# Three quarters of a depthwise convolution moved from VectorE to TensorE, and two thirds of its norm moved to an earlier stage

## The chip, the cores and the metric

The kernel runs on one core of a Trainium2 chip. The metric is the device time in microseconds (us) of one execution. Three runs of the kernel before took 2881.78 us in the median (2876.07 to 2883.0).

## The reference

One step of a two-layer encoder over 1024 prompt tokens and 8 x 16 sample tokens, 1152 in all, model width 1024. Layer 0 has stick-breaking attention (8 heads of 64) and, in parallel, a convolution module over 512 channels; layer 1 has banded attention with 16 heads; each layer is followed by a squared-ReLU MLP of width 4096. Everything is float32. The part that the change touches:

```python
def conv_module(u_ext, dw_w, dw_b, ln_g, ln_b):      # dw_w: 31 taps x 512 channels
    y = lax.conv_general_dilated(u_ext, dw_w[:, None, :], ..., feature_group_count=CONV_CH) + dw_b
    return jax.nn.silu(layernorm(y, ln_g, ln_b))

q, k, v, a, g = jnp.split(h @ w_in, [...])           # ab_project
u = a * jax.nn.sigmoid(g)
u_ext = jnp.concatenate([cache_conv, u], axis=1)      # 30 old rows, zeros for the prompt
out = jnp.concatenate([a_out, c_out], axis=-1) @ w_out
```

The convolution is depthwise: each of the 512 channels has its own 31 taps along the tokens. The layer norm goes over the 512 channels. The last 30 rows of u are outputs too.

## The kernel before

Activations lie with 128 channels on the partitions and the 1152 tokens along the free axis, in three groups of 384 (`G`). A matmul of high precision is made of three fp32r matmuls over a high and a low half of each operand (`SPLIT`); `split` makes the halves, one on ScalarE (L180) and one on VectorE (L181). Weights come through SP's queue into three staging buffers `st` (`staging`, L187), are split into `hl` buffers and used by `dense` (L220). `weights_ahead` keeps one chunk of 128 output channels loaded ahead.

Layer 0's mixer is `mixer0`. `start` loads the tokens, normalises them and projects the first two of the four chunks of u (gate and value). Then comes the projection of head pair 0, and then four rounds, p = 0 to 3. Round p expands q, k and v of its pair, runs 8 jobs of attention (`attend`: scores L864 to L867, sigmoids L868 and L869, a scan and a product on VectorE L847 and L849, transposes L392, splits, weighted sums L404) and the attention of the sample tokens, and has beside it the projection of pair p + 1 as `fill`. Rounds 0 and 1 project also the u chunks 2 and 3 (`ag`); round 3 has instead the first part of the output projection (`part_out`, tiles psoa).

The convolution is `tap`: for each of 4 chunks and 31 taps two VectorE instructions (L671), y = u x w + y, one over the 1024 prompt tokens and one over the 128 sample tokens. There are 124 such steps; `TAPS` shares them out, 26 beside the first projection and 36, 38 and 24 in rounds 0, 1 and 2. The finished chunk goes to DRAM (`cat_d`, L674 and L675). `conv_norm`, in round 3, loads all four chunks of a token group back (L955), takes the mean with plain fp32 matmuls against ones (L961), centres (L963), squares, makes 1/std (`rstd_of`, L258 and L280) and scales, applies SiLU, and splits the result into `cat_t`, from which the output projection reads.

The order is written by two planners. `merge` interleaves lists of `Step`s by their planned TensorE time, so that each list advances in proportion; a step may name another that it comes `after`, with a `lag` in ns. `level` spreads extra VectorE steps (the taps) over a list by planned VectorE time. Each engine then runs its instructions in that order. DMAs issued by `dma` stand in SP's queue, those of `put` in POOL's; both are in order.

Of the kernel before, what the change touches and what calls it, by code (L numbers as in the profile page):

```python
# [15 lines left out]
P = 128  # L16
D = 1024
KC = 8
T = 1152
TP = 1024  # L20
TAPS = (26, 36, 38, 24)
# [10 lines left out]
UW = UP + 8 * US  # L32
NF = 32
# [86 lines left out]
def tile_trunk(ctx, tc, ins, outs):  # L120
# [26 lines left out]
    dw = const.tile([P, 4, CW], F32, name="dw")  # L147
    cvec = const.tile([P, 3, 4], F32, name="cvec")
    for t, n in ((norms, "norms"), (dw, "dw"), (cvec, "cvec")):
        (nc.scalar.dma_start if n == "norms" else put)(t, ins[n])  # L150
# [23 lines left out]
    xr_d = [dram.tile([KC, P, T], F32, name=f"xr_d{l}") for l in range(2)]  # L174
    hid_d = [dram.tile([NF, P, T], F32, name=f"hid_d{l}") for l in range(2)]

# [415 lines left out]
    def mixer0():  # L592
        with ExitStack() as st:
# [28 lines left out]
            us, ys, tapped = {}, {}, [0] * 4  # L622
            conv_pool = ExitStack()
            cv = Bufs(conv_pool.enter_context(pool("conv")), u=2, y=1)

            def gate(c, ps, g):
                if g == 0:
                    assert c < 2 or tapped[c - 2] == CW
                    us[c] = cv.tile([P, UW], F32, "u", f"u{c}")
                    nc.gpsimd.memset(us[c][:, 0:CW - 1], 0.0)  # L630
                    dma(us[c][:, UP:].rearrange("p (b t) -> p b t", t=US)[:, :, 0:CW - 1], ins["conv_in"][:, c])
# [8 lines left out]
            def u_parts(c, ps, g):  # L640
                n = G if g < 2 else TP - 2 * G
                o = CW - 1 + g * G
                parts = [(us[c][:, o:o + n], ps[:, :n], rstd[g][:, :n])]
                if g == 2:
                    parts.append((us[c][:, UP:].rearrange("p (b t) -> p b t", t=US)[:, :, CW - 1:],
                                  ps[:, n:G].rearrange("p (b t) -> p b t", t=16), None))
                return parts

            def value(c, ps, g):
                for dst, src, _ in u_parts(c, ps, g):  # L650
                    tt(dst, src, dst, ALU.mult)
                if g == 2:
                    put(outs["conv_p"][c], us[c][:, TP:UP])
                    put(outs["conv_s"][c], us[c][:, UP:].rearrange("p (b t) -> p b t", t=US)[:, :, 16:])

            def tap(c, j):
                if j == 0:
# [5 lines left out]
                          u[:, UP:].rearrange("p (b t) -> p b t", t=US)[:, :, j:j + 16]))  # L663
# [13 lines left out]
            taps = [Step(0.0, lambda c=c, j=j: tap(c, j), 1340.0) for c in range(4) for j in range(CW)]  # L677
# [225 lines left out]
            run(level(proj(0), taps[:TAPS[0]]))  # L903
            taps = taps[TAPS[0]:]
            carry, cat_t = [], None
            for p in range(4):
                S["p"] = p
                expand_qk(p)
                if p < 3:
                    fill = proj(p + 1)  # L910
                    if p < 2:
                        fill[10:10] = ag(p + 2)
                    n = TAPS[p + 1]
                    mix, now, taps = [], taps[:n], taps[n:]
                else:
                    cat_t = new_hs("cat0")
                    (first, fill), now = part_out(0, range(3), pp, cat_t), []
                    for s in taps:
                        s.pe = 900.0
                    mix = taps + conv_norm(lambda: (conv_pool.close(), Bufs(st.enter_context(pool("ln")), t1=3, yl=5))[1],  # L920
                                           cat_t)
                cat = Cat(0, p, wk, cat_t)
# [15 lines left out]
                run(level(merge(steps, sample, fill, mix), now))  # L938
            return cat_t

    def conv_norm(new_pool, cat_t):

        steps = []
# [3 lines left out]
        def norm(g):  # L947
            box = {}

            def load():  # L950
# [3 lines left out]
                for c in range(4):  # L954
                    put(box["y"][c], cat_d[0][4 + c, :, g * G:g * G + G])  # L955
# [19 lines left out]
            def out(c):  # L975
# [7 lines left out]
                split(cat_t[g][1][0][:, c, :], cat_t[g][1][1][:, c, :], y)  # L983
# [3 lines left out]
                     Step(2600.0, centre, 1900.0, f"c{name}", f"l{name}", 4000), Step(500.0, squares, 1400.0),  # L987
                     Step(700.0, scale, 1200.0, f"s{name}", f"c{name}", 5000),
# [731 lines left out]
```

## Time and profile before

| what | us |
|---|---|
| median of three runs | 2881.78 |
| the profiled execution, whole | 2879.29 |
| its span, first to last instruction | 2877.5 |
| TensorE busy in the span | 2778.7 |
| VectorE busy in the span | 2015.6 |
| ScalarE busy in the span | 1264.4 |

The profile is of one execution. PE is TensorE's matmul, PEld its weight load, DVE is VectorE, ACT ScalarE, POOL GpSimd, and SP the engine that issues most of the DMAs. A matmul's end is modelled, and neighbouring matmuls overlap, so the mean duration of one is longer than the distance between two. The granted clock of TensorE (PEclk) is given as a share of full speed, 2.4 GHz; its other level is half of that.

### The profile page before, as it was taken

What the parts mean: (1) busy time and instruction counts of PE and PEld (TensorE: products, weight loads), DVE (VectorE), ACT (ScalarE), POOL (GpSimd) and SP (SyncE); (2) the same over time, 40 slices, a digit from 0 to 9 for tenths busy, and PEclk for the clock granted to TensorE, in tenths of its full rate; (3) what the DMA queues carried; (4) which work ended last, traced back from release to release, by engine and by line L of the source; (5) the groups of instructions that cost most, each with busy time, mean ns of one, the idle gap of its engine ahead of it and who ended that gap; (6) DMA issues with size and microseconds to landing.
All of it is one profiled execution on the core that took longest, in us unless ns stands there. A gap on an engine that the chain in (4) does not pass through costs nothing.

```text
span 2877.5 us, 48092 instructions
## 1 busy us (share of the span) xinstructions
PE 2778.7 (97%) x18586; PEld 2674.3 (93%) x18586; DVE 2015.6 (70%) x3939; ACT 1264.4 (44%) x2644; POOL 282.3 (10%) x511
## 2 busy tenths in 40 slices
PE   8988988899999999999999999998999999999998
PEld 8987876799999999999999999997999999999998
DVE  8999999988666654444567777778786666644445
ACT  5344446665555531211355555556555554411112
POOL 1000101031000000000111111110310110000001
PEclk9999998999999999999999999999999999999999
DMA  4434346443332362321344444446532322732311
GB/s 152 131 102 127 114 123 205 147 162 117 106 105 94 131 232 77 109 79 46 107 141 133 135 143 139 134 132 220 180 123 94 102 99 102 251 102 67 110 34 66
DMA packets 136004, 357.70 MB, mean 124 GB/s; under 512 B 21232, under 2 KB 44976, under 8 KB 133728
## 3 DMA queue, kind: packets, MB, share of 16 engines
q1 hardware_dynamic: 105936, 252.06, 27.5%
q0 software_dynamic: 29696, 102.56, 10.5%
q8 instruction: 146, 2.39, 0.3%
q14 instruction: 82, 0.67, 0.1%
q10 hardware_dynamic: 144, 0.02, 0.0%
HBM read 252.90 MB, written 89.03 MB: 119 GB/s over the span
## 4 chain that ended last, share of the span: by engine, by line
PE 75%; DVE 16%; ACT 4%; issue 3%; DMA 2%; POOL 0%; DVEq 0%; SPq 0%; ACTq 0%; POOLq 0%
PE pd L1485 28%; PE um L1380 23%; PE psc L220 10%; DVE y L671 4%; DVE kp L847 2%; PE avc L404 2%; PE psoa L220 2%; PE tpc L392 2%; PE f L220 1%; DVE sg L849 1%; PE zc L1137 1%; DVE wla L181 1%; PE zc L1138 1%; PE psp L220 1%; PE zs L505 1%
## 5 line engine op out<-in xcount | busy, mean ns | idle before, releaser
L1489 DVE TENSOR_TENSOR sl<-sl,pd 128x384 f32<-128x384 f32 x384 | 211.6, 552 | 342.4 <-PE pd L1485 342.0
L220 PE MATMUL psc<-h,hl_wc 128*128 128x384 f32 x1728 | 328.2, 340 | 0.0
L220 PEld LDWEIGHTS psc<-h,hl_wc 128*128 128x128 f32 x1728 | 298.5, 189 | 13.4 <-issue 11.5
L1380 PE MATMUL um<-sl,hl_m 128*128 128x288 f32 x1548 | 240.3, 296 | 0.0
L1380 PEld LDWEIGHTS um<-sl,hl_m 128*128 128x128 f32 x1548 | 217.7, 188 | 0.0
L671 DVE SCALAR_TENSOR_TENSOR y<-u,dw,y 128x1024 f32<-128x1024 f32 (+1 forms) x232 | 176.4, 807 | 0.4
L220 PE MATMUL psp<-h,hl_wi 128*128 128x384 f32 x864 | 169.7, 345 | 0.2 <-ACT kps L896 0.2
L220 PEld LDWEIGHTS psp<-h,hl_wi 128*128 128x128 f32 x864 | 150.4, 191 | 6.4 <-issue 4.9
L1485 PE MATMUL pd<-hsm,wdm 128*128 128x384 f32 x864 | 150.8, 334 | 0.0
L1485 PEld LDWEIGHTS pd<-hsm,wdm 128*128 128x128 f32 x864 | 149.9, 188 | 0.0
L181 DVE TENSOR_TENSOR hl_m<-xr,hl_m 128x512 fp32r<-128x512 f32 x132 | 92.4, 700 | 57.1 <-ACT hl_m L180 55.8
L180 ACT ACTIVATE hl_m<-xr 128x512 fp32r<-128x512 f32 x132 | 82.2, 623 | 104.7 <-PE um L1380 83.2
L1387 ACT ACTIVATE hdm<-hdm 128x288 f32<-128x288 f32 x192 | 84.8, 442 | 91.7 <-DVE hdm L1386 90.9
L1380 PE MATMUL um<-sl,hl 128*128 128x288 f32 x756 | 119.4, 296 | 0.0
L1104 ACT ACTIVATE s<-s,mxc 128x640 f32<-128x640 f32 (+4 forms) x128 | 88.8, 694 | 59.8 <-DVE mxc L1101 58.1
L1380 PEld LDWEIGHTS um<-sl,hl 128*128 128x128 f32 x756 | 106.6, 188 | 0.8
L180 ACT ACTIVATE wdm<-st_wd 128x512 fp32r<-128x512 f32 x40 | 23.8, 624 | 171.2 <-PE pd L1485 144.8
L1101 DVE CUSTOM_DVE_ANT_0 s<-zc,bp 128x384 f32<-128x384 f32 (+3 forms) x128 | 66.0, 517 | 38.9 <-PE zc L1138 38.1
L180 ACT ACTIVATE whc<-tpc 128x512 fp32r<-128x512 f32 (+1 forms) x144 | 72.5, 523 | 47.0 <-PE tpc L392 46.1
L181 DVE TENSOR_TENSOR wlc<-tpc,whc 128x512 fp32r<-128x512 f32 (+1 forms) x144 | 83.5, 595 | 12.8 <-ACT whc L180 10.4
L1390 POOL DMA_DIRECT2D hid_d<-hdm x96 | 51.9, 540 | 412.9 <-ACT hdm L1388 334.7
L180 ACT ACTIVATE hl<-st_wd 128x512 fp32r<-128x512 f32 x20 | 12.6, 629 | 171.0 <-PE pd L1485 155.3
(495 smaller groups left out, 6997.6 us busy)
## 6 DMA issues: line engine op xcount, KB each, us to landing
hrm<-hid_d SPq DMA_DIRECT2D x64, 576.0 KB, 5.0
xr<-in_w_up_dram SPq DMA_DIRECT2D x64, 512.0 KB, 3.7
st_wd<-in_w_down_dram SPq DMA_DIRECT2D x128, 256.0 KB, 3.3
hid_d<-hdm POOLq DMA_DIRECT2D x96, 288.0 KB, 2.4
st_wc<-in_w_in_c_dram SPq DMA_DIRECT2D x48, 256.0 KB, 2.7
xm_d<-xo POOLq DMA_DIRECT2D x16, 576.0 KB, 3.5
xr<-xm_d SPq DMA_DIRECT2D x16, 576.0 KB, 4.6
xr_d<-xr POOLq DMA_DIRECT2D x16, 576.0 KB, 3.3
```

The source lines that it names most:

```text
L180: ACT(hi, src, AF.Copy)
L181: return tt(lo, src, f(hi), ALU.subtract)
L220: mm(ps()[:, :G], hl[:, a, at:at + P], act[g][k // 4][b][:, k % 4, :], start=n == 0, stop=n == len(todo) - 1)
L392: nc.tensor.transpose(tp[:, c0 + q * P:c0 + (q + 1) * P], blocks.get(j, tile_q), ident)
L404: mm(st["av"][:, o0:o0 + n], vs[:, j, i].rearrange("p a d -> p (a d)"), src[:, c0:c0 + n], start=st["done"] == 0, stop=st["done"] == nmm - 1)
L671: stt(src if j == CW - 1 else dst, src, wj, dst, ALU.mult, ALU.add)
L1101: nc.vector.tensor_tensor_reduce(s[:, c:c + m], z, b, -1.0, mx, ALU.add, ALU.min, new)
L1104: ACT(s[:, :n], s[:, :n], AF.Exp, bias=mx, scale=-1.0, accum_out=tot)
L1380: mm(banks[b, n][:, :TQ], w[:, a, c * P:c * P + P], combo(key, c)[:, h, n * TQ:n * TQ + TQ], start=k < 3 and c == 0 and i == 0, stop=c == ...
L1387: ACT(y, y, AF.Relu)
L1485: mm(ps[:, :G], w[:, a, c % 4 * P:c % 4 * P + P], hid[NB * j + e][b][:, g * G:g * G + G], start=n == 0, stop=n == 3 * NB - 1)
L1489: tt(xs, xs, ps[:, :G], ALU.add)
```

## The change

- Chunk 0 of u is convolved as before, by 31 taps on VectorE: 26 beside the first projection, 5 at the head of round 0. The 93 steps of chunks 1 to 3 are gone.
- Chunks 1 to 3 are stored by phase: a tile of 8 phases x 180 positions, token t at phase t mod 8, position t div 8, with the old rows of the eight sample streams laid out the same way. So `gate` and `value` write and read these chunks with neighbouring tokens 180 elements apart. The old rows come from a new input `conv_ph` through a staging buffer and a copy on ScalarE; the outputs of the last 30 rows are gathered by two copies on ScalarE.
- Each such chunk goes to DRAM (`u_d`) and is read back with 16 channels x 8 phases on the partitions, in 8 groups (`products.load`).
- `products.one`: per group 5 fp32 matmuls of a 128x128 matrix against 176 columns, shifted by one position each, summed in one bank. The matrices (`dw_t`, 120 in 40 loads of three) hold the taps and are made on the host. Three loads fit in the buffer; a further one is issued when its place has been used up. Two ScalarE instructions add the bias and evict; the chunk goes to DRAM (`y_d`) after its eighth group.
- Chunk 1 is convolved in round 0, chunk 2 in round 1, chunk 3 in round 2, as a list `mix` of its own in `merge`.
- The norm of token groups 0 and 1 follows chunk 3 in round 2; it writes its result to `cat_d`, and `ready_chunks` brings chunks 4 to 7 of these two groups back in round 3. Group 2 stays in round 3. The norm's loads read `y_d` through staging buffers and reorder by a copy on ScalarE. Lags of its steps are longer.
- In rounds 0 and 1 the two extra chunks of the projection come after q and k (place 20) and no longer after q (place 10).

```diff
-TAPS = (26, 36, 38, 24)
+TAPS = 26
...
-                    mine[1:1] = [16 + p + 1, 12 + p + 1]
+                    mine[2:2] = [16 + p + 1, 12 + p + 1]
...
+                o = 4 + g * G // PH
+                parts = [(us[c][:, :, o:o + n // PH].rearrange("p h s -> p s h"),
+                          *(t.rearrange("p (s h) -> p s h", h=PH) for t in (ps[:, :n], r)))]
...
+                put(u_d[c - 1], us[c])
...
-            taps = [Step(0.0, lambda c=c, j=j: tap(c, j), 1340.0) for c in range(4) for j in range(CW)]
+            taps = [Step(0.0, lambda c=c, j=j: tap(c, j), 1340.0) for c in range(1) for j in range(CW)]
+            toep = {}
+
+            def toeplitz(n):
+
+                if n in toep or 3 * n >= 3 * PH * ND:
+                    return
+                if not toep:
+                    toep["all"] = cv.tile([P, T], F32, "y", "toep").rearrange("p (n m) -> p n m", m=P)
+                toep[n] = toep["all"][:, n % 3 * 3:n % 3 * 3 + 3]
+                dma(toep[n], ins["dw_t"][n].rearrange("p (n m) -> p n m", m=P))
+
+            def products(c):
...
+                def load():
+                    assert tapped[0] == CW
+                    r = box["r"] = cv.tile([P, PH * UC], F32, f"u{int(c == 0)}", f"ur{c}").rearrange("p (i s) -> p i s", i=PH)
+                    dma(r, u_d[c].rearrange("(i q) h s -> (q h) i s", q=CG))
+                    for n in range(3):
+                        toeplitz(n)
+
+                def one(i):
+                    r = box["r"]
+                    ps = bank(f"cv{c}{i}")
+                    n = UC - ND + 1
+                    for d in range(ND):
+                        at = (c * PH + i) * ND + d
+                        mm(ps[:, :n], toep[at // 3][:, at % 3], r[:, i, d:d + n], start=d == 0, stop=d == ND - 1)
+                    for n in range(at // 3 + 4):
+                        if 3 * (n - 3) + 2 <= at:
+                            toeplitz(n)
+
+                    b = dwb[:, c, i:i + 1]
+                    ACT(r[:, i, :TP // PH], ps[:, :TP // PH], AF.Identity, bias=b)
+                    ACT(r[:, i, TP // PH:YC].rearrange("p (b s) -> p b s", s=2),
+                        ps[:, 132:UC].rearrange("p (b s) -> p b s", s=6)[:, :, 0:2], AF.Identity, bias=b)
+                    if i == PH - 1:
+                        put(y_d[c].rearrange("(i q) h s -> (q h) i s", q=CG), r[:, :, :YC])
+
+                name = f"ur{c}"
+                return ([Step(50.0, load, 0.0, name)]
+                        + [Step(1500.0, lambda i=i: one(i), 0.0, None, name, 9000) for i in range(PH)])
...
-                        fill[10:10] = ag(p + 2)
-                    n = TAPS[p + 1]
-                    mix, now, taps = [], taps[:n], taps[n:]
+                        fill[20:20] = ag(p + 2)
+                    mix = products(p)
+                    if p == 0:
+                        mix = taps[TAPS:] + mix
+                    if p == 2:
+                        cat_t = new_hs("cat0")
+                        norm_steps = conv_norm(lambda: (conv_pool.close(), Bufs(st.enter_context(pool("ln")),
+                                                                                 t1=3, yl=5))[1], cat_t)
+                        mix += norm_steps[0] + norm_steps[1]
                 else:
...
+                    (first, fill) = part_out(0, range(3), pp, cat_t)
+                    mix = norm_steps[2] + ready_chunks(0, range(4, KC), pp, cat_t, range(2))
+                    for n, s in enumerate(mix[-4:]):
+                        s.after, s.lag = "ready", 8000.0 + 6000.0 * n
...
-                for c in range(4):
-                    put(box["y"][c], cat_d[0][4 + c, :, g * G:g * G + G])
+                put(box["y"][0], cat_d[0][4, :, g * G:g * G + G])
+                n = G // PH
+                for c in range(3):
+                    t = sp.tile([P, 512], F32, "st", f"yp{g}{c}")[:, :G].rearrange("p (h s) -> p h s", h=PH)
+                    put(t, y_d[c][:, :, g * n:g * n + n])
+                    ACT(box["y"][1 + c].rearrange("p (s h) -> p s h", h=PH), t.rearrange("p h s -> p s h"), AF.Copy)
...
-                split(cat_t[g][1][0][:, c, :], cat_t[g][1][1][:, c, :], y)
+                if g < 2:
+                    put(cat_d[0][4 + c, :, g * G:g * G + G], y)
+                else:
+                    split(*(t[:, c, :] for t in cat_t[g][1]), y)
```

## Rows read from the trace of the kernel before

**Rows 1.** The page: span, TensorE's share, then busy tenths in 40 slices.
```profile
span 2877.5 us, 48092 instructions
...
PE 2778.7 (97%) x18586; PEld 2674.3 (93%) x18586; DVE 2015.6 (70%) x3939; ACT 1264.4 (44%) x2644; POOL 282.3 (10%) x511
...
PE   8988988899999999999999999998999999999998
...
DVE  8999999988666654444567777778786666644445
```
**Rows 2.** Windows, pairs 0 to 3: length; PE, PEld, DVE, ACT, POOL busy; clock; DMA.
```profile
94.00:205.00 111.00, 104.27 (x744) 94.75 (x743) 109.31 (x150) 50.73 (x117) 9.91 (x18) 1.00 0.43 129
205.00:330.00 125.00, 113.02 (x782) 99.77 (x781) 122.84 (x174) 52.44 (x120) 12.59 (x22) 0.95 0.40 120
330.00:445.00 115.00, 100.42 (x756) 86.35 (x754) 114.50 (x156) 55.98 (x127) 12.21 (x22) 0.96 0.46 135
445.00:585.00 140.00, 120.35 (x791) 98.04 (x790) 126.01 (x226) 94.33 (x204) 12.64 (x24) 0.91 0.51 166
```
**Rows 3.** Windows of line L671, the taps: DVE busy in pairs 0 to 2.
```profile
94.00:205.00 111.00, 51.70 (x64) 1.00 0.43 129
205.00:330.00 125.00, 55.93 (x74) 0.95 0.40 120
330.00:445.00 115.00, 45.04 (x60) 0.96 0.46 135
```
**Rows 4.** Waits of PE, 62 to 590 us: total, times, longest.
```profile
PE ava L404 <- DVE wla L181: 14.6, 17, 2.5
PE tpa L392 <- DVE sg L849: 7.9, 10, 1.9
```
**Rows 5.** Windows of layer 1: two pairs, and the last one.
```profile
1660.00:1800.00 140.00, 136.85 (x1011) 128.90 (x1010) 103.28 (x290) 76.08 (x176) 18.03 (x42) 1.00 0.46 137
...
1940.00:2040.00 100.00, 91.12 (x614) 83.58 (x613) 78.87 (x221) 55.12 (x133) 8.37 (x17) 0.95 0.63 210
```
**Rows 6.** Windows of line L220: PE and PEld busy in pair 3 and layer 1.
```profile
445.00:585.00 140.00, 53.24 (x238) 42.57 (x238) 0.91 0.51 166
1660.00:1800.00 140.00, 81.94 (x433) 73.77 (x432) 1.00 0.46 137
```
**Rows 7.** Timeline of PE: mean, then sums of squares and rows of 1/std.
```profile
464.14 2.85 PE L961 MATMUL mu<-yl,ones 128*128 128x384 f32 x8
...
522.63 0.76 PE L258 MATMUL ms_l<-ones,sq_l 128*128 128x1 f32 x6
...
527.44 0.91 PE L280 MATMUL rr_l<-sq_l,ones 128*128 128x384 f32 x2
```
**Rows 8.** Line L961: duration ns min, median, max; first and last start.
```profile
L961 PE MATMUL mu<-yl,ones x24: 484/486/842, 464.1 to 551.1; 128*128 128x384 f32 x24
```
**Rows 9.** Line L654, a store of 1,024 pieces; weight loads' size and landing, 60 to 600.
```profile
L654 POOL DMA_DIRECT2D out_conv_s_dram<-u x4: 894/898/902, 61.5 to 305.4; - x4
...
DMA to landing us min/median/max: 5.1/6.1/6.5
...
st_wi<-in_w_in_ab_dram SPq DMA_DIRECT2D x27, 256.0 KB, 3.2
```
**Rows 10.** Windows of pair 3 for tiles yl, sq_l (five columns or four), cr (DVE, ACT).
```profile
445.00:585.00 140.00, 9.05 (x24) 4.86 (x24) 23.52 (x46) 26.70 (x47) 5.14 (x10) 0.91 0.51 166
...
445.00:585.00 140.00, 6.57 (x24) 3.53 (x24) 6.96 (x18) 6.00 (x12) 0.91 0.51 166
...
445.00:585.00 140.00, 4.48 (x9) 4.03 (x9) 0.91 0.51 166
```
**Rows 11.** Waits of SP's queue, 94 to 445 us: total, times, longest.
```profile
SPq L476 <- PE so L539: 98.5, 10, 19.2
```
**Rows 12.** Line L636, the gate's first VectorE instruction: duration ns min, median, max.
```profile
L636 DVE TENSOR_TENSOR u<-psg,rh x4: 527/540/551, 137.3 to 273.8; 128x384 f32<-128x384 f32 x4
```
**Rows 13.** Groups of VectorE, 94 to 445 us: the splits of projection weights.
```profile
L181 DVE TENSOR_TENSOR hl_wi<-st_wi,hl_wi 128x512 fp32r<-128x512 f32 x25 | 16.6, 681 | 0.9 <-ACT hl_wi L180 0.9
```

More of the change, by code (lines that the diff above doesn't have):

```diff
@@ L32 @@
 UW = UP + 8 * US
+PH = 8
+UC = 180
+YC = T // PH
+CG = 16
+ND = 5
 NF = 32
@@ L174, in tile_trunk @@
     xr_d = [dram.tile([KC, P, T], F32, name=f"xr_d{l}") for l in range(2)]
+    u_d, y_d = ([dram.tile([P, PH, n], F32, name=f"{t}_d{c}") for c in range(3)] for t, n in (("u", UC), ("y", YC)))
     hid_d = [dram.tile([NF, P, T], F32, name=f"hid_d{l}") for l in range(2)]
@@ L902, in mixer0 @@
             vs = pp.tile([P, 8, 2, 2, HD], F32R, "vs", "vs0")
-            run(level(proj(0), taps[:TAPS[0]]))
-            taps = taps[TAPS[0]:]
+            run(level(proj(0), taps[:TAPS]))
+            for s in taps[TAPS:]:
+                s.pe = 400.0
             carry, cat_t = [], None
@@ L937, in mixer0 @@
                 sample = two_samples(*(sample_steps(0, p, bg, S, wk, load, soft, cs) for bg in range(2)))
-                run(level(merge(steps, sample, fill, mix), now))
+                run(merge(steps, sample, fill, mix))
             return cat_t
     def conv_norm(new_pool, cat_t):
-        steps = []
         pools = []
@@ L982, in out, with ready_chunks @@
                 tt(y, y, s, ALU.mult)
[L983 removed]
+                if g < 2:
+                    put(cat_d[0][4 + c, :, g * G:g * G + G], y)
+                else:
+                    split(*(t[:, c, :] for t in cat_t[g][1]), y)
             name = f"ln{g}"
             return ([Step(50.0, load, 0.0, f"l{name}"),
[L987 to L996 removed]
+                     Step(3900.0, centre, 2200.0, f"c{name}", f"l{name}", 7000),
+                     Step(0.0, squares, 1700.0, None, f"c{name}", 3000),
+                     Step(1300.0, scale, 1200.0, f"s{name}", f"c{name}", 9000),
+                     Step(970.0, lambda: box["rows"](), 0.0, f"r{name}", f"s{name}", 5000)]
+                    + [Step(300.0, lambda c=c: out(c), 1500.0, f"o{name}", f"r{name}", 1500) for c in range(4)])
+        return [norm(g) for g in range(NG)]
+    def ready_chunks(layer, chunks, pp, cat_t, groups=range(NG)):
         steps = []
@@ L1001, in go @@
                 cr = pp.tile([P, T], F32, "sk", f"cr{layer}{c}")
-                dma(cr, cat_d[layer][c])
-                for g in range(NG):
+                n = len(groups) * G
+                dma(cr[:, :n], cat_d[layer][c, :, :n])
+                for g in groups:
                     hi, lo = (x[:, c % 4, :] for x in cat_t[g][c // 4])
```

85 lines of the change are left out of this document (55 added, 30 removed).

## The prediction

> **What bounds the kernel now.** I read the page's busy shares and 40 slices first. TensorE is busy 97% of the span; the slices below nine are all among the first nine, in layer 0's mixer, and there VectorE stands at eight or nine [rows 1]. The rest of the span is not touched by the change, so only that stretch matters. Cut by stage (busy time by windows), the four head pairs run from 94 to 585 us: pair 0 from 94 to 205, pair 1 to 330, pair 2 to 445, pair 3 to 585, by the first score matmul of each and the stretch in which its last weights are used. VectorE is busy 109.3 + 122.8 + 114.5 + 126.0 = 472.7 of these 491 us, 96% [rows 2]. The taps are 51.7 + 55.9 + 45.0 = 152.7 us of that, in the first three pairs alone; pair 3 has none [rows 3]. What ends TensorE's idle time there is VectorE: the low half of the attention weights (L181) 14.6 us and the product after the scan (L849) 7.9 us are the two longest [rows 4]. So VectorE is the bound of pairs 0 to 3, and TensorE is next, close behind. How close decides everything, because the change moves work from the one to the other.
>
> How much room has TensorE? By matmul busy time 104.3 + 113.0 + 100.4 + 120.4 = 438.1 of 491 us, 53 us idle; by weight loads 94.8 + 99.8 + 86.4 + 98.0 = 378.9 us, 112 us idle [rows 2]. A stretch that shows what a dense mixer looks like on this chip is layer 1: two pairs in 140 us, VectorE at 103.3 us (74%), granted clock 1.00, weight loads 128.9 us, that is 92.1%. Its last pair, which like pair 3 has the output projection beside it and waits for its own results, reaches 83.58 of 100 us [rows 5]. The matmuls of one form tell which measure is honest: those of L220 take 81.94 / 433 = 189 ns of busy time each in layer 1, but 53.24 / 238 = 224 in pair 3, where the clock was 0.91 and many stand alone; by weight loads it is 170 and 179 [rows 6]. Busy time of matmuls swells where TensorE waits, so I count by weight loads.
>
> The Trainium skill (Perfetto Trace Analysis, Identifying the Most-Contended Engine) says the same in general: matmul busy share is no measure of headroom, the weight loads' share is. The trace bears it out by the numbers just given. By the measure that it warns of, the sum comes out near zero, and that is rival B.
>
> **The change, part by part.**
>
> *Taps.* 93 of 124 taps go, two instructions each. 198 instructions took 152.7 us, 0.77 us each [rows 3]; 186 x 0.77 = 143 us leave VectorE in pairs 0 to 2. The first 26 taps stay beside the first projection, the other 5 of chunk 0 stand first in pair 0. VectorE then has 346.6 - 143 = 204 us of 351, 58%, plus the moved norm below: the same side of TensorE as in layer 1. So TensorE is late next.
>
> *Products.* 3 chunks x 8 groups of 16 channels x 5 shifts = 120 matmuls of 128x128 by 176 columns in plain fp32. Each such matmul is two instructions here: the mean of the conv norm is 4 matmuls and shows 8. Eight of 384 columns took 2.85 us, the last lasting 0.486, so (2.85 - 0.49) / 7 = 0.338 us apart [rows 7, 8]; in proportion 176 columns take 0.155 us, and 240 x 0.155 = 37.2 us are added to TensorE. The lower bound is this. The upper bound has the weight load exposed: six one-column matmuls of L258 need 0.76 us, 0.127 each [rows 7], so 240 x 0.282 = 67.7 us. I take 37.2, since the eight of the mean have their weight loads hidden and 0.155 is longer than 0.127. Nothing hides it if TensorE is the bound; it is on the path. ScalarE gets 48 evictions and some 20 copies; it is busy under half the time (50.7 of 111 us in pair 0 [rows 2]), and none of them is waited for by more than the chain below.
>
> *Pairs 0 to 2.* Their weight loads, 280.9 us, at layer 1's density 0.921 take 305.0 us. Add 37.2 of products and the two norm groups that move in: 2.85 + 0.76 + 0.91 = 4.5 us each [rows 7], 9.0 together. The first of these groups waits for a chain: the last eviction, the store of y (1,024 pieces; the comparable store of 1,024 pieces takes 0.9 us to issue and 6.1 to land [rows 9]), three loads of the same kind on the same queue, three copies: about 15 us, against a planned lag of 7. Other steps cover part of it; between 0 and 8 us I take 5. Sum 305.0 + 37.2 + 9.0 + 5 = 356 us against 351: 5 us **lost**. TensorE at density 0.921 plus the products is just as long as VectorE with its taps.
>
> *Pair 3.* Two of three norm groups leave. VectorE has 23.52 + 6.96 = 30.5 us on their tiles, two thirds 20.3; what comes back is eight splits out of the reloaded chunks at 4.48 / 9 = 0.50, 4.0 us [rows 10]. VectorE goes from 126.0 to 109.7 us; at the pairs' present share 0.963 that is 114 us. By TensorE: weight loads on those tiles 4.86 + 3.53 = 8.4, two thirds 5.6; (98.0 - 5.6) / 0.836, layer 1's last pair, is 110.6. I take the longer, 114: 26 us **gained**. Bounds: 110 (VectorE at pair 0's 0.985) to 122 (at its present 0.90).
>
> *Queues.* SP gets 40 loads of shift matrices (192 KB each) and 3 of u. From the fourth on, a load of matrices waits until TensorE has used up the third before it, and weights and caches are queued behind it. SP already waits like this, 98.5 us in total for TensorE before the value caches [rows 11], while TensorE is dense. Because each new wait ends at matmuls issued just before it, I cost it at nothing; without that cover it is rival D. POOL's norm loads wait for y, with attention outputs queued behind; their buffers are two, the wait some 6 us, inside the 5 above. The staging buffers lent to the norm loads and to the conv state cost nothing while weights are a chunk ahead. The later place of the two extra chunks in pair 0's and 1's order: nothing, the same matmuls.
>
> *Strided access.* Gate and value of chunks 1 to 3 now step 180 elements between neighbours in SBUF. The trace has runs of 16 and 64 elements, none of single ones. 24 VectorE instructions at 0.55 [rows 12] are 13 us; between no price and double, I take none, since VectorE has room, except in the start, where a third of them stand: 0 to 4 us.
>
> The Trainium skill (SBUF — State Buffer, Door 1: The DMA port swizzle) says that accesses crossing to a new 16-byte line each time pay a penalty. No row here shows such a pattern; if it doubled these instructions the start would be 4 us longer, and that is rival E.
>
> Total: +5 - 26 = -21 us on an execution of 2879.29 us (span 2877.5): 2858. The runs' median, 2881.78, lies 2.5 above that, so the forecast is **2860 us**, its own range 2845 to 2873.
>
> **Rivals.** A is the forecast.
> B, *TensorE is already full*: by matmul busy, pairs 0 to 2 are 317.7 us of work; at layer 1's 136.85 / 140 = 0.978 that is 325, plus 46 is 371, 20 us more; pair 3 shrinks by 20 or 26. Change 0 to -6: 2876 to 2882. For it: TensorE 94% busy in pair 0. Against: the swollen matmuls.
> C, *TensorE gets denser than layer 1*: VectorE keeps a little more room than there, so 0.95 instead of 0.921 (296 us) and no chain wait: -35, 2846, or 2838 with pair 3 at 110 and a shorter handover. For it: in pairs 1 and 2 the clock stood at 0.95 and 0.96 and would stay up. Against: pair 0, whose clock was 1.00 throughout, reached only 94.75 / 111 = 0.854 [rows 2], and layer 1 had VectorE no busier than this would be.
> D, *SP held up, slower*: a matrix load stands at the head of SP's queue until TensorE has passed it; the next weights behind it come late, and each late chunk costs the landing, 3.2 us [rows 9], and at least VectorE's half of the split, 0.68 [rows 13]. There are 3 + 2, 3 + 2 and 3 = 13 weight chunks in pairs 0 to 2: all late is 13 x 3.9 = 51 us, 2911. It decides from 6 late chunks on (23 us). For it: 43 new loads in an in-order queue. Against: weights are issued a chunk, over 12 us, ahead.
> E, *strides are dear*: double price, 4 us at the start and no more, 2864; at four times, 13 us there, 2873.
>
> **How the numbers follow.** This kernel's runs tell 0.3% (8.6 us) from no change: below 2873 is faster, above 2890 slower. A 0.52, C 0.13, B 0.14, E 0.07, D 0.14. Faster: A, C, most of E, and little of B: 0.71. Same: most of B and some of E: 0.13. Slower: D and the products' upper bound within B: 0.16. Range 2835 to 2884: low end C, high end B; beyond lie D and a tail of C.
>
> **What would show it.** Right: VectorE under 75% in pairs 0 to 2, weight loads near 90% with the products' own, these three pairs within 10 us of their old length, pair 3 near 114 us, all gain there; products 0.15 us apart. Wrong: pairs 0 to 2 more than 15 us shorter (then C); matmul waits ended by DMA of weights or by SP (D); products at 0.28 apart; gate instructions at 1.1 us (E); pair 3 as long as before, because attention's own chain, not VectorE's load, sets it.

## The result, and the profile after

| kernel | median, us | range of the runs | ratio to before, 95% |
|---|---|---|---|
| before | 2881.78 | 2876.07 to 2886.45 (5 runs) | |
| after | 2891.6 | 2890.63 to 2895.8 (5 runs) | 1.0037 (1.0023 to 1.0051) |

The change makes the kernel about 10 us slower, where 2860 was forecast. The profiled executions differ by 12.3 us of span. The page of the changed kernel, for [rows 1]: span, busy time, then busy tenths in 40 slices.

```profile
span 2889.8 us, 48602 instructions
...
PE 2794.3 (97%) x18826; PEld 2706.2 (94%) x18826; DVE 1902.0 (66%) x3753; ACT 1289.6 (45%) x2710; POOL 290.3 (10%) x520
...
PE   8999996899999999999999999998999999999998
...
DVE  8966567888666664444567777778786666644445
```

VectorE lost 114 us of work, and on TensorE the seventh slice, 433 to 506 us, is now a six where it was an eight. Where that time lies is read by marks that every kernel here has: the first transposes of v of pairs 0 to 3, and the first matmul of the second part of the output projection (psob). The windows of [rows 2] do not begin where the pairs do: the first score matmuls of pairs 0 to 3 in before are these.

```profile
105.33 0.22 PE L864 MATMUL z<-k,q 128*128 128x128 f32 x1
...
239.79 0.28 PE L864 MATMUL z<-k,q 128*128 128x128 f32 x1
...
363.25 0.22 PE L864 MATMUL z<-k,q 128*128 128x128 f32 x1
...
475.43 0.31 PE L864 MATMUL z<-k,q 128*128 128x128 f32 x1
```

So before is cut anew. Windows, before and then after; columns as in [rows 2].

```profile
105.00:240.00 135.00, 124.88 (x903) 111.15 (x903) 133.15 (x183) 58.38 (x131) 12.77 (x23) 0.99 0.45 135
240.00:363.00 123.00, 112.02 (x787) 98.16 (x787) 120.81 (x170) 56.54 (x129) 11.14 (x19) 0.96 0.38 114
363.00:476.00 113.00, 94.99 (x659) 78.85 (x658) 108.18 (x152) 57.69 (x134) 12.27 (x22) 0.89 0.49 148
476.00:580.00 104.00, 90.23 (x632) 75.12 (x631) 94.91 (x177) 73.97 (x161) 8.13 (x15) 0.95 0.48 159
```
```profile
104.00:238.00 134.00, 133.19 (x988) 122.32 (x987) 88.86 (x115) 64.67 (x152) 12.78 (x23) 1.00 0.60 175
238.00:359.00 121.00, 117.28 (x879) 108.81 (x879) 77.78 (x102) 62.53 (x151) 12.17 (x21) 1.00 0.53 156
359.00:493.00 134.00, 105.27 (x748) 90.54 (x748) 90.11 (x142) 84.28 (x183) 22.32 (x35) 0.89 0.53 155
493.00:589.00 96.00, 81.50 (x606) 70.77 (x605) 85.02 (x148) 61.75 (x142) 4.84 (x9) 0.96 0.54 176
```

By the marks themselves (windows are rounded to 1 us), in us:

| stretch | before | after | after, norm load later | after, norm back in pair 3 |
|---|---|---|---|---|
| start | 107.8 | 106.6 | 107.1 | 110.8 |
| pair 0 | 132.3 | 131.9 | 131.8 | 131.9 |
| pair 1 | 123.4 | 120.7 | 120.7 | 116.8 |
| pair 2 | 112.3 | 133.6 | 120.4 | 103.1 |
| pair 3, to psob | 104.2 | 96.0 | 99.4 | 108.9 |
| psob to the MLP | 64.7 | 63.9 | 64.3 | 65.6 |

The third and fourth columns are e1_load_late and e3_norm_back below. Pairs 0 and 1 are what was forecast: VectorE at 66% and 64%, TensorE's weight loads at 122.32 / 134 = 91% and 108.81 / 121 = 90%, nearly the old length. Pair 2 is 21.3 us longer, and there TensorE's weight loads are at 68%. Pair 3 is only 8.3 us shorter. Of the rest, about 4 us lie at the start of the MLP. There after's TensorE ran part of the time at half clock (granted 0.82 of 2.4 GHz between 670 and 680 us, against 1.00 before). From the first matmul of the MLP to the end, which no edit touches, the profiles of the kernels in this document take 2232.8 (before) to 2243.8 us (e3), so I put these 4 us down to no edit; no run tests that.

In pair 2 one place stands out. A window of after at the handover to pair 3, then the longest waits of TensorE in 359 to 493 us (total, times, longest), its timeline, and then those of POOL, ScalarE and SP.

```profile
460.00:480.00 20.00, 5.01 (x15) 3.81 (x16) 12.62 (x29) 15.34 (x27) 2.77 (x5) 0.50 0.46 136
```
```profile
PE psoa L227 <- ACT hl_wo0a L187: 10.6, 1, 10.6
...
PE st L532 <- ACT kp L947: 4.6, 1, 4.6
...
PE rr_l L287 <- DVE sq_l L283: 4.4, 1, 4.4
```
```profile
465.79 1.91 PE L399 MATMUL tpa<-ident,sg 128*128 128x128 f32 x8
...
478.34 4.21 PE L227 MATMUL psoa<-cat,hl_wo0a 128*128 128x384 f32 x12 [10.63 <-ACT hl_wo0a L187]
```
```profile
436.50 0.91 POOL L1040 DMA_DIRECT2D yp<-y_d  x1
...
471.66 1.14 POOL L1070 DMA_DIRECT2D cat_d<-yl  x2 [9.78 <-DVE yl L1068]
```
```profile
474.07 1.58 ACT L1041 ACTIVATE yl<-yp 128x384 f32<-128x384 f32 x2
...
477.76 0.52 ACT L187 ACTIVATE hl_wo0a<-st_wo0a 128x384 fp32r<-128x384 f32 x1
```
```profile
474.94 7.85 SPq L194 DMA_DIRECT2D st_wo0a<-in_w_out_ab_dram  x7
```

Read from the end: the first output projection starts at 478.34 after 10.63 us of idleness, because its weights were split at 477.76, because they were issued only at 474.94. In the kernel before SP began to send them 114 us earlier:

```profile
360.55 0.49 SPq L187 DMA_DIRECT2D st_wo0a<-in_w_out_ab_dram  x1
...
388.67 1.52 SPq L187 DMA_DIRECT2D st_wo0a<-in_w_out_ab_dram  x2
```

The staging buffers `st` are three. The norm load of token group 2, first step of round 3, takes all three of them. They come free when ScalarE's three copies (L1041) have read them; the first of these copies needs a `yl` buffer, five in all, that group 1 still holds until POOL has sent its result to `cat_d` (471.66 us). So the weights wait for the copies, the copies for stores, the stores for VectorE's last step of group 1. SP's own waits in 380 to 500 us name it:

```profile
SPq L194 <- ACT yl L1041: 11.6, 3, 9.7
```

### The profile page after: what moved, and what is told of

Its sections match the earlier page's. It is cut to its first block, busy times and chain, and to the rows that moved or that the text cites. A ratio compares the mean times of both kernels' runs of the same rounds, so it can differ in the third digit from the quotient of the medians.

```text
span 2889.8 us, 48602 instructions
## 1 busy us (share of the span) xinstructions
PE 2794.3 (97%) x18826; PEld 2706.2 (94%) x18826; DVE 1902.0 (66%) x3753; ACT 1289.6 (45%) x2710; POOL 290.3 (10%) x520
## 4 chain that ended last, share of the span: by engine, by line
PE 72%; DVE 6%; issue 4%; ACT 3%; DMA 2%; POOL 0%; DVEq 0%; ACTq 0%; POOLq 0%; SPq 0%
PE pd L1574 27%; PE um L1469 24%; PE psc L227 10%; PE avc L411 2%; PE tpc L399 2%; PE zc L1226 1%; PE zc L1227 1%; PE psob L227 1%; PE psoa L227 1%; DVE kp L925 1%; PE so L546 1%; DVE xr L1392 1%; DMA xm_d<-xo 0%; PE zs L512 0%; DMA hrm<-hid_d 0%
## 5 line engine op out<-in xcount | busy, mean ns | idle before, releaser
L1578 DVE TENSOR_TENSOR sl<-sl,pd 128x384 f32<-128x384 f32 x384 | 212.0, 553 | 342.4 <-PE pd L1574 342.2
L925 DVE TENSOR_TENSOR_SCAN kp<-kp,ones 128x128 f32<-128x128 f32 (+3 forms) x64 | 86.5, 1353 | 40.4 <-ACT kp L947 40.0
L1469 PEld LDWEIGHTS um<-sl,hl 128*128 128x128 f32 x756 | 106.6, 188 | 0.8
```

Of the source, the lines that this page charges most:

```text
L925: nc.vector.tensor_tensor_scan(keep[:, 0:n][:, ::-1], keep[:, 0:n][:, ::-1], ones[:, 0:1].to_broadcast([P, n]), 1.0, ALU.mult, ALU.mult)
L1469: mm(banks[b, n][:, :TQ], w[:, a, c * P:c * P + P], combo(key, c)[:, h, n * TQ:n * TQ + TQ], start=k < 3 and c == 0 and i == 0, stop=c == ...
L1578: tt(xs, xs, ps[:, :G], ALU.add)
```

## The experiments

The questions were: is the wait for the weights what makes pair 2 long (S), or the norm's own chain, wherever it stands (N)? Is pair 3 bound by VectorE (V), as forecast, or by TensorE's work and its chains (T)? Are pairs 0 to 2 full on TensorE (F)? And does a norm that starts late end late, so that what pair 2 gains is given back behind it (L)? All ratios are to the kernel before, with 95% intervals; its median was 2881.8 to 2882.7 us in every series of runs.

**e1_load_late.** The norm load of group 2 gets a lag, so that the weights are staged ahead of it.
```diff
                         s.after, s.lag = "ready", 8000.0 + 6000.0 * n
+                    mix[0].after, mix[0].lag = "ready", 5000.0
```


> The changed kernel, with the load step of the norm of token group 2 planned behind the third reloaded chunk of round 3 (after ready, lag 5000) and no longer at the head of round 3. Theory S (staging): the norm's loads hold the three staging buffers at the handover from pair 2 to pair 3, so the first weights of the output projection, issued at 474.9 us, are late, and TensorE waits 10.6 us for them. Without that hold the first psoa matmul comes at 462 to 470 us in place of 478, and the whole is 8 to 12 us shorter than the changed kernel: 2880 to 2884. Rival F (TensorE full): the products' 37 us on TensorE are the loss and the wait is only where it shows; less than 4 us shorter. Rival N (norm chain): the norm's own chain in round 2 (copies, 1/std, 4.4 us of waiting for L287) is the loss; psoa moves by less than 5 us.

Measured: 2884.07 us, 1.0014 (1.0003 to 1.0025). Rows of SP and TensorE:
```profile
436.56 0.33 SPq L194 DMA_DIRECT2D st_wo0a<-in_w_out_ab_dram  x1
```
```profile
466.82 1.30 PE L227 MATMUL psoa<-cat,hl_wo0a 128*128 128x384 f32 x6
```
The 10.6 us wait is gone. Pair 2 shrinks by 13.2 us, pair 3 grows by 3.4, and the median falls by 7.5: most of the loss goes with the wait for the weights, a little less than S forecast. (The lag also puts the norm of group 2 later; the run does not separate the two.) But pair 2 stays 8.1 us longer than before, with the 4.4 us waits of L532 and L287 still there.

**e2_own_buffer.** The same wait taken away in another way: the norm's loads go through one buffer of their own.
```diff
-                                                                                 t1=3, yl=5))[1], cat_t)
+                                                                                 t1=3, yl=5, yp=1))[1], cat_t)
...
-                    t = sp.tile([P, 512], F32, "st", f"yp{g}{c}")[:, :G].rearrange("p (h s) -> p h s", h=PH)
+                    t = pools[0].tile([P, G], F32, "yp", f"yp{g}{c}").rearrange("p (h s) -> p h s", h=PH)
```


> The changed kernel, with the norm's loads of y in one buffer of their own (the norm's pool has room for one) and no longer in the three staging buffers. Theory S: no staging buffer is held by the norm, the first weights of the output projection are issued before 460 us, the first psoa matmul comes at 462 to 470 us, and the whole is 8 to 15 us shorter: 2877 to 2884. Theory F: less than 4 us shorter. Theory N: one buffer makes the norm's loads follow one another, about 6 us each, so the norm in round 2 takes some 10 us more and the whole is the same or up to 10 us longer than the changed kernel.

Measured: 2892.21 us, 1.0037 (1.0024 to 1.005), no gain. The weights were issued at 345 us, but with one buffer load and copy take turns, and TensorE waits for the chain instead (waits of PE, 359 to 491 us):
```profile
PE mu L1047 <- ACT yl L1041: 7.4, 4, 3.2
```
The first output matmul comes at 473.5 (after: 478.3). So taking the wait for the weights away is not enough: what lengthens the norm's chain is paid in TensorE's waits for it, as N said.

**e3_norm_back.** The products stay, the norm of groups 0 and 1 goes back beside pair 3, and its result is split directly as before.
```diff
-                        mix += norm_steps[0] + norm_steps[1]
...
-                    mix = norm_steps[2] + ready_chunks(0, range(4, KC), pp, cat_t, range(2))
-                    for n, s in enumerate(mix[-4:]):
-                        s.after, s.lag = "ready", 8000.0 + 6000.0 * n
+                    mix = norm_steps[0] + norm_steps[1] + norm_steps[2]
...
-                if g < 2:
+                if g < 0:
```


> The changed kernel, with the norm of all three token groups in round 3 and its result split straight into the projection's operand, as before the change; the products stay in rounds 0 to 2. Theory S: no norm load stands at the handover before the first output weights, so pair 2 ends as early as its products allow (first transposes of v in pair 3 at 478 to 486 us in place of 492.8), but pair 3 has the old norm load again (104 us and more in place of 96): the whole 2884 to 2892, about as long as the changed kernel. Theory F: 2890 to 2894, pair 2 as long as now. Theory N: pair 2 shrinks by 15 us or more, to under 119, and the whole is at 2882 or less.

Measured: 2878.01 us, 0.9989 (0.9977 to 1.0). Windows of its pairs 2 and 3:
```profile
359.50:462.60 103.10, 92.77 (x716) 82.99 (x714) 71.47 (x97) 60.75 (x145) 12.93 (x21) 0.95 0.53 162
462.60:571.50 108.90, 94.57 (x649) 81.35 (x649) 99.00 (x183) 79.18 (x172) 9.51 (x14) 0.91 0.50 163
```
This is N's forecast. Moving two groups out of pair 3 shortens it by 9.5 us with the load late (108.9 against 99.4 in e1) and by 12.9 as the change does it (96.0), not by 26; moving them into pair 2 costs 17.3 there even with the load late (103.1 against 120.4), and 30.5 as the change does it. The 17.3 are about the 9.0 of TensorE's own work and the two waits of 4.4, which e3's pair 2 does not have; this sum is argued, not tested. So the norm's move is a loss, and the products without it are worth about 5 us, with an interval that reaches to nothing. (The profile is of a run of 2882.67 us, above the median. In it pairs 0 to 3 are together 11.5 us shorter than before; the start is 3.0 longer and all behind psob 11.9.)

**e4_one_shift.** After, with one of the five shifts of each product; the convolution is left incomplete.
```diff
-                        mm(ps[:, :n], toep[at // 3][:, at % 3], r[:, i, d:d + n], start=d == 0, stop=d == ND - 1)
+                        mm(ps[:, :n], toep[at // 3][:, at % 3], r[:, i, d:d + n], start=d == 0, stop=d == 0) if d == 0 else None
```


> The changed kernel with one of the five shifted matmuls of each product (the first); the other four are left out, so the convolution of chunks 1 to 3 has only part of its taps. All loads, evictions and the norm stay. 192 matmul instructions fewer at 0.15 us are 29 us. Theory F: TensorE is the bound of pairs 0 to 2, nearly all of it comes back, 24 to 29 us: 2863 to 2868. Theory S: pairs 0 and 1 shrink by 8 to 10 us each, pair 2 keeps its wait for the weights, 16 to 22 us in all: 2870 to 2876. Theory N: the same as S in pairs 0 and 1, and nothing in pair 2.

Measured: 2870.77 us, 0.9962 (0.9951 to 0.9972). 64 instructions less in each of pairs 0 to 2 are 9.9 us at 0.155; pair 0 lost 9.3 and pair 1 12.2, pair 2 only 3.7. Pairs 0 and 1 are full on TensorE: there each product is paid in full. Pair 2 of the changed kernel is not, its waits stay.

**e5_back_late.** e3, with the norm load behind the handover.
```diff
                     mix = norm_steps[0] + norm_steps[1] + norm_steps[2]
+                    mix[0].after, mix[0].lag = "ready", 0.0
```


> The variant with all of the norm back in round 3 (2878.0 us), and with the first norm load planned behind the third reloaded chunk and not at the head of round 3. Theory S (the norm's loads hold the staging buffers ahead of the output projection's first weights, here until 443 us): the first weights are staged before 440 us, the 3.7 us wait of TensorE for their split goes, 3 to 6 us shorter: 2872 to 2875. Rival L: the norm itself is now last in pair 3, and a later load makes it end later: the same or up to 5 us longer, 2878 to 2883.

Measured: 2879.48 us, 0.9994 (0.9983 to 1.0004). Pair 2 99.8 instead of 103.1, pair 3 117.0 instead of 108.9. The weights come early, and what pair 2 wins pair 3 gives back and more, as L said.

**e6_copies_later.** e1, with ScalarE's three copies as a step of their own behind the load, so that ScalarE is not held by a copy whose data has not landed (theory Q: that this hold makes what is left of pair 2's growth).
```diff
-                    ACT(box["y"][1 + c].rearrange("p (s h) -> p s h", h=PH), t.rearrange("p h s -> p s h"), AF.Copy)
+                    box["t", c] = t
+
+            def copies():
+                for c in range(3):
+                    ACT(box["y"][1 + c].rearrange("p (s h) -> p s h", h=PH), box["t", c].rearrange("p h s -> p s h"), AF.Copy)
...
+                     Step(0.0, copies, 0.0, f"y{name}", f"l{name}", 9000),
...
```


> The variant with the norm of groups 0 and 1 in round 2 and group 2's load late (2884.1 us), and with ScalarE's copies of the loaded y in a step of their own, planned 9 us after the loads, so that they do not stand in ScalarE's queue while the loads are under way. Theory Q (queue): attention's sigmoids stood behind those copies (TensorE waits 4.4 us at L532 for a sigmoid); that wait goes and pair 2, 120.4 us, shrinks to 114 to 117: 2878 to 2881. Rival N (the norm's chain as such, 1/std and the handover without other work): the 4.4 us at L287 stay, pair 2 stays within 2 us: 2883 to 2886.

Measured: 2889.31 us, 1.0027 (1.0017 to 1.0038), 5 us slower than e1 and slower than either forecast. Waits of PE, 94 to 600 us:
```profile
PE ms_l L265 <- DVE sq_l L301: 7.3, 1, 7.3
...
PE st L532 <- ACT kp L947: 4.7, 2, 4.3
```
The wait of L532 is as long as before, and a later step of the norm now waits 7.3 us. But this does not refute Q, for the edit did not take the hold away. ScalarE and POOL in after, with the landing of L751's three stores, and then ScalarE in this run:
```profile
393.86 0.90 ACT L1041 ACTIVATE yl<-yp 128x384 f32<-128x384 f32 x1
399.10 0.85 ACT L1041 ACTIVATE yl<-yp 128x384 f32<-128x384 f32 x1 [4.34 <-issue]
...
400.33 0.59 ACT L947 ACTIVATE kp<-z 128x512 f32<-128x512 f32 x1
...
L1041 ACTq EVENT_SEMAPHORE  x8: 17/17/6050, 392.9 to 476.2; - x8
```
```profile
372.24 0.93 POOL L1040 DMA_DIRECT2D yp<-y_d  x1 [12.85 <-DMA ct02v<-in_sb_v_dram]
...
391.12 0.93 POOL L751 DMA_DIRECT2D y_d<-ur  x1 [6.51 <-ACT ur L748]
...
DMA to landing us min/median/max: 5.0/5.9/7.9
```
```profile
398.50 0.85 ACT L1046 ACTIVATE yl<-yp 128x384 f32<-128x384 f32 x1 [4.05 <-issue]
```
In both kernels the second copy of group 0 keeps ScalarE idle for over 4 us, and the sigmoids that make `kp`, whose scores were done at 392.9 us in after, stand behind it; TensorE's wait ends with them, at 400.97. The copy's data was there (its load was issued at 372.24). Its semaphore wait, the longest of the line at 6.05 us, ended when the store of chunk 3's products, issued at 391.12, had landed 7.9 us later. The norm's buffers are opened in the place of the convolution's, so the copy's target probably lies where that store still read. In e6 the copy waits for the same store, however late it is planned behind its load. So ScalarE is held, as Q had it, but by a store and not by the load; no run takes this hold away.

**e8_no_stride.** e3, with gate and value of chunks 1 to 3 written to neighbouring elements; the tokens then stand in another order than the products expect.
```diff
-                parts = [(us[c][:, :, o:o + n // PH].rearrange("p h s -> p s h"),
-                          *(t.rearrange("p (s h) -> p s h", h=PH) for t in (ps[:, :n], r)))]
+                parts = [(us[c][:, :, o:o + n // PH],
+                          *(t.rearrange("p (h s) -> p h s", h=PH) for t in (ps[:, :n], r)))]
```


> The variant with all of the norm back in round 3 (2878.0 us), and with gate and value of chunks 1 to 3 reading and writing neighbouring elements: the prompt tokens of a group are stored unsorted, so the convolution mixes the wrong tokens. In the changed kernel's trace the strided instruction takes 0.93 us on VectorE in place of 0.55 and 0.98 on ScalarE in place of 0.53; 20 of the one and some 9 of the other become short: 12 us of engine time. Theory F (TensorE is the bound of pairs 0 and 1): only the start is shorter, 0 to 4 us: 2874 to 2878. Rival V (VectorE's and ScalarE's chains still set pairs 0 to 2): 6 to 12 us shorter, 2866 to 2872.

Measured: 2875.94 us, 0.9973 (0.9963 to 0.9983), 2 us less than e3, within what the two intervals leave open. The strides cost little on the path.

**e7_two_chunks.** e3, with two chunks by taps and two by products: 26 taps beside the first projection, 24 spread over round 0, 12 at the head of round 1; products of chunk 2 in round 1 and of chunk 3 in round 2.
```diff
+NT = 2
...
-                    mix = products(p)
-                    if p == 0:
-                        mix = taps[TAPS:] + mix
+                    mix = products(p - 1) if p else []
+                    if p == 1:
+                        mix = taps[TAPS + 24:] + mix
...
-                run(merge(steps, sample, fill, mix))
+                run(level(merge(steps, sample, fill, mix), taps[TAPS:TAPS + 24] if p == 0 else []))
```


> The variant with all of the norm back in round 3 (2878.0 us), and with chunk 1 convolved by taps on VectorE again: 26 taps beside the first projection, 24 beside round 0, 12 at the head of round 1; products only for chunk 2 in round 1 and chunk 3 in round 2. TensorE loses 12.4 us of products in round 0, VectorE gets 31 taps, 48 us, 29 of them more than now in round 0. Theory F: pair 0 is bound by TensorE and has about 45 us of VectorE's time free; it shrinks from 132 to 120 to 124 us, pair 1 stays within 3 us of 117, and the whole is 2866 to 2871. Rival V: VectorE, at 118 of 122 us, is the bound of pair 0 again; it shrinks by less than 4 us and the whole is 2874 to 2879.

Measured: 2872.43 us, 0.9969 (0.9956 to 0.9982): faster than before and than after, the best of the kernels that compute everything. Its pairs 0 and 1:
```profile
107.00:234.00 127.00, 120.01 (x883) 108.08 (x881) 118.86 (x161) 59.20 (x130) 11.13 (x20) 0.97 0.53 151
234.00:356.00 122.00, 116.30 (x872) 106.54 (x871) 85.10 (x112) 60.99 (x148) 13.51 (x23) 1.00 0.55 162
```
Pair 0 is 4.4 us shorter than e3's, with VectorE at 118.86 of 127 and TensorE's weight loads at 85%: between what F and V said, since both engines are nearly full.

**e9_norm_no_pe and e10_norm_less_dve.** e3 twice: once without TensorE's part of the norm (mean, sums of squares, rows of 1/std), once without 13 of 15 wide VectorE instructions of each group (VectorE's busy time fell by 16.5 us in all, from 1898.7 to 1882.2).
```diff
-                for c in range(4):
-                    mm(mu[:, :G], ones, yl[c], start=c == 0, stop=c == 3)
...
-        for j in range(NG):
+        for j in range(0 if no_pe else NG):
```
```diff
-                for c in range(4):
-                    stt(yl[c], mu[:, :G], -1.0 / 512, yl[c], ALU.mult, ALU.add)
+                stt(yl[3], mu[:, :G], -1.0 / 512, yl[3], ALU.mult, ALU.add)
...
-                tt(y, y, s, ALU.mult)
```


> The variant with all of the norm back in round 3 (2878.0 us; pair 3 lasts 108.9 us from its first transposes of v to the first psob), with TensorE's part of the three norm groups left out: the centring, the variance and the rows of 1/std read other data of the same size, so the norm's values are not a norm's. VectorE and ScalarE do all that they did. Theory T (pair 3 is bound by TensorE and the chains on it, so the norm there costs its TensorE time): pair 3 shrinks by 9 to 14 us, to 95 to 100, the whole is 2864 to 2870. Theory V (VectorE is the bound of pair 3, as the prediction had it): under 4 us, 2874 to 2878.

> The variant with all of the norm back in round 3 (2878.0 us), with 13 of VectorE's 15 wide instructions of each norm group left out (centring of three chunks, the sums of squares, the products with 1/std and with the sigmoid), 39 x 0.55 = 21.5 us; TensorE's and ScalarE's part stays, the norm's values are not a norm's. Theory V: pair 3 (108.9 us) shrinks by 13 to 21 us, the whole is 2857 to 2866. Theory T: it shrinks by 5 us or less, 2872 to 2878.

Measured: e9 2864.86 us, 0.9941 (0.9926 to 0.9955); e10 2873.03 us, 0.9965 (0.995 to 0.998). Windows of pair 3, e9 and then e10:
```profile
457.00:556.40 99.40, 82.56 (x612) 69.66 (x611) 96.31 (x179) 78.83 (x172) 9.83 (x15) 0.98 0.54 178
```
```profile
460.70:569.30 108.60, 93.72 (x649) 80.30 (x649) 84.09 (x149) 78.68 (x171) 8.90 (x14) 0.92 0.49 162
```
Against e3's pair 3 (108.9 us, VectorE 99.00), VectorE's work falls by 14.9 us in e10 and the pair stays as it is; in e9 VectorE keeps its work, is busy 97%, and the pair is 9.4 us shorter. T, not V. Pairs 2 and 3 together say the same: 212.0 us in e3, 213.2 in e10, 201.3 in e9. (e9 takes away TensorE's work and the waits on its results together; the two were not separated. The median of e10 is 5 us under e3's, and no pair of the profiles accounts for that. e3's profile is 9.8 us longer than e10's, in its start, 110.8 against 105.9 us, and behind the pairs, which the edit does not touch.)

**e11_two_late.** e7, with e5's edit.
```diff
                     mix = norm_steps[0] + norm_steps[1] + norm_steps[2]
+                    mix[0].after, mix[0].lag = "ready", 0.0
```


> The version with chunks 0 and 1 by taps and chunks 2 and 3 by products (2872.4 us), and with the first norm load of round 3 planned behind the third reloaded chunk. Theory S: the staging buffers go to the output projection's weights first, psoa starts some 5 us earlier (440 in place of 445) and the whole is 0 to 4 us shorter, 2868 to 2872. Rival L: the norm, later by as much, ends pair 3 later: 2872 to 2876.

Measured: 2878.27 us, 0.9988 (0.9979 to 0.9997), 6 us slower than e7 and beyond what L forecast; pair 3 116.7 instead of 106.4. L again: the norm beside pair 3 has to start early.

**e12_back_one_shift.** e3, with e4's edit.

> The variant with all of the norm back in round 3 (2878.0 us) with one of the five shifted matmuls of each product, so the convolution of chunks 1 to 3 has part of its taps only; 29 us less for TensorE. With the norm still in round 2, four shifts less were worth 9.3 us in pair 0, 12.2 in pair 1 and 3.7 in pair 2. Theory F (without the norm in it, pair 2 is bound by TensorE like the other two): pair 2 (103.1) shrinks by 8 to 11 us too, the whole is 2848 to 2854. Rival H: the handover to pair 3, which has no other work for TensorE, sets pair 2's end; it shrinks by less than 5 us, 2855 to 2860.

Measured: 2851.63 us, 0.9894 (0.9879 to 0.9908), 26.4 us under e3, as F forecast for the whole: pairs 0, 1 and 2 are 9.3, 6.8 and 6.1 us shorter, pair 2 between what F and H said. Four shifts are 192 instructions, 29.8 us at 0.155; the three pairs give back 22.2 of it.

## Why the prediction was wrong

The sum said -21 us, the span grew by 12.3. Of these 33 us, 13 lie in pairs 0 to 2 (+18.2 where +5 stood), 18 in pair 3 (-8.3 where -26 stood) and 2.5 outside the pairs. These are the two failed steps below.

**Right: the taps.** VectorE fell to 66, 64 and 67% in pairs 0 to 2, and TensorE was late next. VectorE's busy time fell by 114 us over the span, less than the 143 of the sum.

**Right: the products' price and place.** The timeline of after:
```profile
127.80 1.65 PE L741 MATMUL cv<-ur,toep 128*128 128x176 f32 x10
```
Ten with the last lasting 0.31: (1.65 - 0.31) / 9 = 0.149 us apart, against 0.155 taken. They lie on the path in pairs 0 and 1 (e4), and their sum there came out as forecast: TensorE at 0.90 to 0.91 by weight loads, layer 1's density, and the two pairs within 3 us of their old length. So C did not come, and neither did B: counting by weight loads was the right measure where TensorE has work in every list.

**Right: SP's hold by matrices (D).** Products waited for a matrix load once, for 1.3 us:
```profile
PE cv L741 <- DMA toep<-in_dw_t_dram: 1.3, 1, 1.3
```

**Wrong: "the staging buffers lent to the norm loads and to the conv state cost nothing while weights are a chunk ahead".** This is the first failed step, 13 us of pair 2. The condition held for the weights of the projections, not for the first weights of round 3: the lent buffers come free only through ScalarE's copies, and these hang on `yl` and so on the stores of the group before. D had late weights in an in-order queue, but with the wrong holder, and 3.9 us for each late chunk where one wait took 10.6. e1 shows it: the wait goes and 7.5 us of the total come back with one lag. e2, where the wait goes at the price of a slower norm, gains nothing.

**Wrong: "I take the longer, 114: 26 us gained".** This is the second failed step and the larger one. The share of VectorE in pair 3, 126.0 of 140 [rows 2], was read as its bound. e10 shows that 14.9 us less of VectorE's work change nothing there, and e9 that TensorE's side of the norm does. By the marks, pair 3 won 8.3 us by losing two groups (the first of them began at 464.14 us [rows 7], so a part of it stood ahead of pair 3), and 9.4 in e9 against e3 by losing TensorE's part of all three. And even by VectorE 8 of the 26 had no ground in pair 3: the sum divided by the share of all pairs, 0.963; at pair 3's own, 0.90, the same 109.7 us give the 122 of its upper bound, 18 gained. The prediction's own last sentence, that attention's chain and not VectorE's load might set pair 3, was named as what would refute it, but no rival was priced on it: the rival on the slower side should have been this one. Read so, the move is an exchange, TensorE time from pair 3 to pair 2.

**Too small: the 5 us for the norm's chain in pair 2, of "between 0 and 8".** Beyond the staging, pair 2 pays 17.3 us for two groups (e1 against e3), where 9.0 + 5 stood. The waits L532 and L287 are 4.4 each. The first comes at 401 us, in mid-pair, and contradicts the sentence on ScalarE that none of its copies is waited for by more than the chain: it had time to spare, but its queue stood behind one copy that had to wait (rows in e6).

**Strides: right that they cost nothing much, wrong that their price is none.** Lines of after: an instruction of the gate on VectorE, ScalarE's sigmoid beside it, and the reordering copies; then the first two lines without strides, in e8.
```profile
L652 DVE TENSOR_TENSOR u<-u,rh x8: 556/926/943, 32.1 to 287.7; 128x384 f32<-128x384 f32 x8
...
L651 ACT ACTIVATE u<-u x8: 525/983/985, 31.1 to 285.8; 128x384 f32<-128x384 f32 x8
...
L1041 ACT ACTIVATE yl<-yp x9: 829/854/901, 393.9 to 476.9; 128x384 f32<-128x384 f32 x9
```
```profile
L652 DVE TENSOR_TENSOR u<-u,rh x8: 525/556/561, 32.2 to 286.8; 128x384 f32<-128x384 f32 x8
...
L651 ACT ACTIVATE u<-u x8: 507/524/527, 31.4 to 284.9; 128x384 f32<-128x384 f32 x8
```
0.93 us against 0.56: 1.7 times, near E's price, but the start did not grow (106.6 against 107.8) and e8 gives back 2 us in all. The Trainium skill (SBUF — State Buffer, Door 1: The DMA port swizzle) says that accesses that step to a new 16-byte line each time pay; these rows agree.

**Readings that do not hold, and change little.** The windows of [rows 2] begin 11 to 35 us ahead of the first score matmuls that they are said to begin with, so 445 to 585 us holds the last 30 us of pair 2; VectorE's share is the same by the marks (94.91 of 104 us, 0.91). The slices of TensorE below nine are not all among the first nine: the 28th and the last are eights too [rows 1], outside the stretch that changed. And 109.7 us at 0.985 are 111.4, not the 110 of the lower bound.

The sum, by the marks: pairs 0 and 1 -3.1, pair 2 +21.3, pair 3 -8.3, start -1.2, all behind it +3.7: +12.4 against +12.3 of span. Forecast were +5 for pairs 0 to 2 and -26 for pair 3.

## What to carry to other kernels

A high busy share names a bound only where the engine's work, taken away, shortens the stretch; before moving work out of a stretch, price each engine's part of it, and expect back only the part of the engine that sets the length. Taking 117 us of busy time off VectorE bought about 5 us here (e3), because TensorE was close behind it and got 37 us more of weight loads; sharing the work so that both engines are nearly full (e7) bought 10. A pool of buffers that an in-order queue of weights runs ahead through is not free to lend: the loan lasts as long as the slowest consumer's own output buffers. And an engine with time to spare still holds up others when an instruction that has to wait stands ahead of theirs in its queue.

## What the runs showed of the hardware

Elements 720 bytes apart in SBUF cost both engines: VectorE 0.93 us for 384 elements, ScalarE 0.98, where the same lines took 0.56 and 0.52 in e8 with neighbouring elements. In the mixers that were read here, by pairs, TensorE's weight loads took at most 0.93 of the time, in layer 1 of the kernel before (130.32 of 140 us), and 0.91 in layer 0 (after's pair 0), products included:
```profile
1520.00:1660.00 140.00, 137.74 (x1015) 130.32 (x1014) 101.69 (x286) 74.80 (x173) 17.44 (x41) 1.00 0.46 144
```
That this is the share to count with for a mixer is an estimate from these stretches; in the first projection (62 to 94 us of before) it was 32.00 of 32. A store of 1,024 pieces landed 5.0 to 7.9 us after its issue (L751 of after). Where TensorE idled (5.01 of 20 us busy at 460 to 480 us) the granted clock was 0.50, 1.2 GHz, and the twelve matmuls that ended the wait took 4.21 us, 0.35 each, where six of the same took 1.30, 0.22 each, in e1 with the clock granted in full.
